# The second half of each low-part subtraction stays on the Pool engine up to the end of the cross attention

## The chip, the cores and the metric

One NeuronCore of a Trainium2 chip runs the whole program. The metric is the device time of one execution in microseconds (us); the number for a kernel is the median of its runs. Engine names are those of the profile: PE is the matrix engine (PEld its weight loads), DVE the vector engine, ACT the scalar engine, POOL the general-purpose engine, SP the engine that issues most of the transfers.

## What is computed

One layer of a transformer-like network on 256 tokens of 1024 channels, in float32:

```
x = layer_norm(ALPHA * x + token_mixer(x))        # three branches, gated and summed:
                                                  #   sparse attention, convolution, gated linear attention
x = layer_norm(ALPHA * x + cross_attention(x, mem))
x = layer_norm(ALPHA * x + moe_ffn(x))            # 32 experts, 4 for each token
```

The token mixer multiplies x by `w_in` (1024 x 6952), each branch's result by a 512 x 1024 matrix, and the gated sum by `w_out`; the cross attention has projections for queries, keys, values and its output. The experts hold 32 x 3 matrices' worth of 1024 x 1024 weights, 12 MB each expert.

## The kernel before

**Stages.** The program has a front, which is the token mixer and the cross attention, and then the experts. In the front every weight is used in blocks of 512 rows by 512 columns, 1 MB each, called slots here. A block comes by a transfer into one of six places of a ring (`fetch`, `R0 = 6`), is cut in two parts, and is multiplied by the activations, which are cut in two as well: three products stand for one float32 product (high times high, high times low, low times high).

**One slot** (`wslot`, line 121). The block `t` is [128, 4, 512]. It is handled in two halves, j = 0 (its first two chunks of 128 rows) and j = 2 (its last two). For each half ACT copies it to `wh` in a format of fewer bits, and then `t - wh` is written to `wl` by one subtraction of 128 x 1024 elements:

```
for j, eng in ((0, self.nc.vector), (2, self.nc.gpsimd if self.pooled else self.nc.vector)):
    js = slice(j, j + 2)
    self.copy(h[:, js, :n], t[:, js, :n])
    eng.tensor_tensor(out=l[:, js, :n], in0=t[:, js, :n], in1=h[:, js, :n].bitcast(F32), op=ALU.subtract)
```

The subtraction of the first half is always DVE's. That of the second half is POOL's where `self.pooled` is set, and DVE's elsewhere (line 142 in both cases). The first slot of the program (`quick`) and the two slots with `pair` don't take this path. `wh` and `wl` have two buffers each, so a slot's copies start when PE is done with the slot two before, and the slot before is multiplied meanwhile. The ring's place of `t` is free when the last of the four instructions has read it; SP then issues the next transfer into it.

**Where pooled is set.** It is 0 from the start, 1 for `nsa_in` (lines 1519 to 1521), whose four plain slots thus use POOL, and 0 again for all that follows: the three calls of `merge` (18 slots), `out_proj` with `w_out` (4), `keys`, `queries` and `values` (12), and `out_proj` with `xa_wo` (4, the last into the tiles `lasth`, `lastl`). That is 38 slots.

**Order.** The instructions of the front are put in an order for each engine by a planner that works through a modelled time: of what is ready on an engine, the one of the highest priority goes first, and program order gives the priority unless `high_priority` lifts it. The splitting of slots is lifted by 3000 places (`PRIO`), the softmaxes of the sparse attention by 6000. Each engine then works through its list strictly in order. From `route` on (line 853), after the slots of `xa_wo`, the order is that of the program.

**Beside the slots.** DVE does three quarters of the 31 taps of the convolution (line 320), with POOL the last quarter (lines 317 and 318), then the convolution's LayerNorm (PE lines 330, 337 and 342 with DVE lines 331, 343 and POOL's power on line 230), the sparse attention's softmaxes (lines 607 to 620), the merges (102, 689), and the LayerNorm after `w_out` (725, 237, 239, 229, POOL's power on 230, 243, 245). The transposes of that LayerNorm's rows on PE (line 91, `row`) lead to the queries. POOL also issues some transfers: the bias table `wide` (271), the LayerNorm's factors `gb` (207), the experts' biases `ye` (1036) and the router's weights `rw` (811). The experts' weights come by SP's queue on lines 1017 and 1024, the first of them while the front still runs, into places of the ring and into the front's memory as it becomes free.

Of the kernel before, what the change touches and what calls it, by code (L numbers as in the profile page):

```python
# [40 lines left out]
NEG = -1.0e30  # L41
# [5 lines left out]
# the first weights' column, in w_in  # L47
GATE0 = 1816
# the expert that comes first, and the place in the sequence of the last LayerNorm's preparation
FIRST = 16  # L50
MID = 20
# pieces of the last LayerNorm: (on DVE, tokens, columns), and of the output
# [4 lines left out]
class Rows:  # L57
    """[128 tokens, 2, 1024] in four tiles of 512 columns"""
# [12 lines left out]
class Front:  # L71
    """The two attention-like sublayers, up to the tokens that the experts see."""
# [23 lines left out]
    def gate(self, out, in_, scale=1.0):  # L96
        """out = 2 * sigmoid(scale * in_) - 1, from the table that has exp too"""
        return self.nc.scalar.activation(out, in_, AF.Tanh, scale=scale / 2)

    def gated(self, out, gate, in_):  # L100
        """out = 2 * sigmoid * in_"""
        self.nc.vector.scalar_tensor_tensor(out, gate, 1.0, in_, op0=ALU.add, op1=ALU.mult)

    def fetch(self, w, r0, c0, n, heads=False, parts=1):
        t = self.ring.tile([P, 4, 512], F32, name="w")
        at = 0
        for a, m in c0 if isinstance(c0, tuple) else ((c0, n),):
            if heads:
                # rows by (head of a group, group, channel)
# [11 lines left out]
    def wslot(self, w, r0, c0, n, pair=False, into=None, heads=False):  # L121
        """512 rows x n columns of a weight, as its 12-bit part and the rest."""
        t = self.ahead.pop() if self.ahead else self.fetch(w, r0, c0, n, heads)
        h, l = into or (self.wsp.tile([P, 4, 512], F32R, name=name) for name in ("wh", "wl"))
        if self.after:
            # the first weights are split after x
            self.copy(h[0:1, :, 0:1], self.after.pop().bitcast(F32))
        with self.tc.high_priority(offset=PRIO):
            if self.quick:
                # the first ones in parts, so that the products start early  # L130
# [14 lines left out]
    def project(self, w, c0, n, outs, x, nslots=2, pair=False, small=False, heads=False):  # L145
        """outs: (bank, offset, 'T', columns) gives [128 channels, 256 tokens];
        (bank, offset, 'N', columns, t) gives [128 tokens, channels]."""
# [3 lines left out]
        banks = []  # L151
# [28 lines left out]
    def projT(self, w, c0, x, nslots=2, pair=False, small=False, heads=False):  # L180
        """512 columns of x @ w, transposed: two banks of [128, 2, 256]."""
        return self.project(w, c0, 512, [(m // 2, (m % 2) * S, 'T', self.col(m * P)) for m in range(4)], x, nslots, pair, small, heads)
# [4 lines left out]
    def to_T(self, nat, nk, pool=None, name=None, into=None):  # L187
        """[128, 2, nk*128] tokens -> [128 channels, nk, 256] split in two."""
# [15 lines left out]
    def bcast_rows(self, dst, src):  # L204
        """every partition of dst gets the row src (n elements)"""
# [4 lines left out]
    def consts(self, cst, keep):  # L210
# [4 lines left out]
        # the PE's clock rises while x comes  # L215
# [10 lines left out]
    def rpow(self, pool, out, in_, eps, n):  # L226
        """out = (in_ + eps) ** -0.5 for [128, n]"""
# [4 lines left out]
    def norm(self, pool, r, out, gb):  # L232
        """LayerNorm of [128, 1024] rows"""
# [13 lines left out]
    def rel_table(self, pool):  # L247
        """skewed copies of the bias: wide[p, h, w] = bias of head h at distance 128 + p - w, NEG where negative"""
# [25 lines left out]
    def conv_cols(self, tmp, pool):  # L274
# [12 lines left out]
        # the taps meet twice the gated values  # L287
# [17 lines left out]
    def conv_out(self, pool):  # L305
        """the taps, a quarter of them on Pool, and the rest of the branch"""
# [73 lines left out]
    def misc_in(self, keep, pool):  # L380
        """the low-rank decay inputs (16) and the gates of the sparse attention (24)"""
# [44 lines left out]
    def gla(self, pool, opool):  # L426
# [5 lines left out]
        # the blocks of 64 on the diagonal  # L432
# [90 lines left out]
    def nsa_in(self, pool):  # L523
# [29 lines left out]
        # compressed keys and values  # L553
# [31 lines left out]
    def nsa(self, pool, opool, wide):  # L585
# [6 lines left out]
        def weights(t, br, g):  # L592
            """the softmax, times the gate"""
# [57 lines left out]
        # the softmax of a part runs before the one before it is turned  # L651
# [41 lines left out]
    def out_proj(self, w, o, enter=None, after={}, into=None):  # L693
        """o @ w, [128 tokens, 512] in bank t * 2 + c; the first tokens are ready before the others"""
# [27 lines left out]
    def residual(self, res, bank, t, c):  # L722
        """res = alpha * res + what the sublayer gave"""
# [9 lines left out]
    def four(self, out, banks, **kw):  # L733
        """two banks of a projection, channels first"""
# [15 lines left out]
    def weights(self, pool, q, kT, pr):  # L750
        """the softmax of the queries against the keys"""
# [38 lines left out]
    def mixed(self, xo, v, pt):  # L790
        """the values by those weights"""
# [11 lines left out]
class Moe:  # L803
# [3 lines left out]
    def prepare(self, cst, pool):  # L807
        """the router seen from rows r before their LayerNorm: logits = rs * (r @ gw - mean * sum(gw)) + (b @ rw + rb)"""
# [27 lines left out]
        # slots from 1 on  # L836
        self.io = cst.tile([P, P], F32, name="io")
        nc.gpsimd.iota(self.io[:], pattern=[[1, P]], base=1, channel_multiplier=0, allow_small_or_imprecise_dtypes=True)
        # rows of an expert, and of a half for each half of the columns
# [13 lines left out]
    def route(self, cst, wk, w, o, into, enter, r, x2h, row):  # L853
        """the last projection of the cross attention, LayerNorm of the rows r, which are in x1's place, but for the
        columns' factors and terms, and beside it what the router makes of them. Its result is in two parts; each tile
        of the second takes the place of the tile of r before it."""
# [32 lines left out]
        def scores(t):  # L889
            # in the PE's column groups, side by side  # L890
# [5 lines left out]
        def busy():  # L896
            """keeps the PE's clock up while it waits"""
# [15 lines left out]
        def largest(t):  # L913
            """the four largest of each token, equal ones by index"""
# [42 lines left out]
        # position of a token among its expert's, from 1; 0 for no token  # L957
# [23 lines left out]
    def residual(self, gb, x2):  # L981
        """the second LayerNorm's result again, for the sum; its factors and terms are brought from columns to rows"""
# [16 lines left out]
    def last_rows(self, gb, rows):  # L999
        """the last LayerNorm's factors and terms, for all partitions"""  # L1000
# [11 lines left out]
    def load(self, e, last=False):  # L1012
        """an expert's weights, in the order in which they are used: rows of w_gu by 128, then of w_down by 256"""
# [15 lines left out]
    def biases(self, pool):  # L1029
        """the experts' biases of g and u, for 128 rows = (half, part, expert)"""  # L1030
# [7 lines left out]
    def setup(self, cst):  # L1038
        """the biases of g and u in two exact parts"""
# [14 lines left out]
    # A block is a run of w slots (64 or 32) of one expert. The outputs' column chunks go to the PE's column groups.  # L1054
    # Slots 0..63 of two experts share the tiles of 128 rows: one gather and one sum for both.
# [7 lines left out]
    def onehot(self, pe, parts):  # L1063
        """slots' one-hot columns, [128 tokens, slots] twice; parts: (expert, first slot, count, column)"""
# [6 lines left out]
    def take(self, pe, xn, c):  # L1071
        """half of the channels of the slots' tokens"""
# [15 lines left out]
    def scaled(self, out, in_, d, on_dve):  # L1088
        """the LayerNorm's factors and terms, for the channels of a run of 128"""
# [6 lines left out]
    def gather_T(self, pe, xT, xT1, j):  # L1096
        """256 of the channels of the first four experts' slots, channels first"""
# [16 lines left out]
    def gates(self, pe, parts, tag="pg"):  # L1114
        """gated one-hot map of slots, in 128 columns; parts: (expert, first of pe's columns, column, count)"""
# [14 lines left out]
    def gates_of(self, e, pe, w):  # L1130
        """for a block that is summed alone: its rows are (column half, slot), with w = 32 all of it twice"""
# [8 lines left out]
    def up(self, e, W, blocks, gus, between=(), lag=0):  # L1140
        """blocks: (xT, w); w = 64: g and u in a bank each, [128 = (half, slot), 512]; w = 32: both in one,
        [128 = (g or u, half, slot), 512]; a second block may lag by some rows of 128"""
        nc = self.nc
        at = 4
# [3 lines left out]
        if blocks[-1][1] != CAP:  # L1148
            # the same for 64 rows, with 64 zeros on each side
# [32 lines left out]
    def act(self, gu, w, uc):  # L1182
        """(u + 1) * g * sigmoid(1.702 g), clamped, in two halves"""
# [41 lines left out]
    def down(self, W, blocks, between=()):  # L1225
        """blocks: (hT, w, bank); w = 64: [128 = (column half, slot), 512]; w = 32: (column half, part of the sum, slot)"""
# [12 lines left out]
    def combine(self, pgT, ye, alone=False, last=False):  # L1239
        """y += the slots' results, by gate; ye: rows are a pair's slots, or (column half, slot) of one block"""  # L1240
# [443 lines left out]
```

## Time and profile before

| what | value |
|---|---|
| median of 3 runs | 1567.79 us |
| the runs | 1559.61, 1567.79, 1568.36 us |
| the profiled execution: span from the first to the last instruction | 1554.9 us |
| span below the fastest run / below the median | 4.7 / 12.9 us |
| PE busy | 1371.5 us (88% of the span) |
| DVE busy | 547.6 us (35%) |
| ACT busy | 320.0 us (21%) |
| POOL busy | 136.6 us (9%) |
| subtractions on line 142 by DVE / by POOL | 98 / 4 |

The page gives the profiled execution by its span alone, so it is set against the runs by the difference in the table. Busy shares are means over stages of very different kinds; the rows below are therefore taken by stretches of the span. A matrix instruction's length in the rows is that from its start to its modelled end, and they overlap: the distance of their starts tells how fast PE goes.

### The profile page before, as it was taken

To read this page: it belongs to the slowest core of one execution; us is meant where nothing else is said; L and a number is where in the kernel's file an instruction comes from. 1 tells how busy PE (TensorE), PEld (TensorE's weight loads), DVE (VectorE), ACT (ScalarE), POOL (GpSimd) and SP (SyncE) were. 2 spreads that over 40 slices of the span, in tenths; PEclk is the share of its full clock that TensorE was granted. 3 is DMA by queue.
4 is the path that set the end of the run, shared out by engine and by line. 5 is a ranking of instruction groups with operands and counts; after the bars stand their busy time and mean duration, and the time that the engine had idled before them with its cause. 6 is when DMAs were issued, how large, how long until landed. Compare 5 with 4: busy or idle time off the path is not lost. (4 is left out here: it accounts for less than half of the span.)

```text
span 1554.9 us, 18456 instructions
## 1 busy us (share of the span) xinstructions
PE 1371.5 (88%) x7190; PEld 705.8 (45%) x7190; DVE 547.6 (35%) x1243; ACT 320.0 (21%) x638; POOL 136.6 (9%) x139
## 2 busy tenths in 40 slices
PE   8879999999999978887879788988888999988895
PEld 8768879998743323232322232223223332233332
DVE  5999785765431221111212121213122122112213
ACT  4424653445320111010101010101111011101100
POOL 3983000000110000000000000000030000000001
PEclk9989999999999998999999899999999999799998
DMA  9436536557789999989996789588889997699970
GB/s 308 138 94 152 188 82 215 205 186 273 273 310 404 414 416 402 405 346 374 365 391 240 297 361 409 220 341 348 355 324 388 417 409 323 252 360 396 384 295 29
DMA packets 110163, 469.93 MB, mean 302 GB/s; under 512 B 12081, under 2 KB 16276, under 8 KB 77244
## 3 DMA queue, kind: packets, MB, share of 16 engines
q1 hardware_dynamic: 108028, 462.53, 76.5%
q0 software_dynamic: 1712, 4.26, 1.3%
q8 instruction: 104, 1.70, 0.4%
q10 hardware_dynamic: 272, 1.05, 0.2%
q14 instruction: 47, 0.39, 0.1%
HBM read 466.49 MB, written 1.31 MB: 301 GB/s over the span
## 5 line engine op out<-in xcount | busy, mean ns | idle before, releaser
L1158 PE MATMUL g<-w,xT 128*64 128x512 f32 x1024 | 299.0, 638 | 52.2 <-issue 27.7
L1158 PE MATMUL u<-w,xT 128*64 128x512 f32 x1024 | 292.4, 619 | 11.4 <-issue 11.4
L1233 PE MATMUL m<-w,hT 128*64 128x512 f32 (+1 forms) x1120 | 253.0, 627 | 0.1
L1192 DVE TENSOR_SCALAR gc<-g 128x256 f32<-128x256 f32 x64 | 26.8, 419 | 520.3 <-PE g L1158 477.1
L1158 PEld LDWEIGHTS g<-w,xT 128*64 128x64 f32 x1024 | 77.7, 144 | 195.6 <-issue 188.2
L1158 PEld LDWEIGHTS u<-w,xT 128*64 128x64 f32 x1024 | 86.7, 144 | 165.6 <-issue 165.6
L1193 ACT ACTIVATE row<-gc 128x256 f32<-128x256 f32 (+1 forms) x70 | 29.1, 417 | 559.8 <-DVE gc L1192 559.8
L142 DVE TENSOR_TENSOR wl<-w,wh 128x1024 fp32r<-128x1024 f32 (+1 forms) x96 | 114.3, 1226 | 66.3 <-ACT wh L80 66.1
L1233 PEld LDWEIGHTS m<-w,hT 128*64 128x64 f32 (+1 forms) x1120 | 73.1, 139 | 134.7 <-issue 132.1
L80 ACT ACTIVATE wh<-w 128x1024 fp32r<-128x1024 f32 (+1 forms) x112 | 105.7, 990 | 101.3 <-PE big L172 65.5
L172 PE MATMUL big<-xh,wh 128*128 128x256 f32 x352 | 101.4, 288 | 0.0
L172 PE MATMUL big<-xl,wh 128*128 128x256 f32 x352 | 101.1, 287 | 0.0
L172 PE MATMUL big<-xh,wl 128*128 128x256 f32 x352 | 100.8, 288 | 0.0
L1401 DVE COPY ye<-m 64x512 f32<-64x512 f32 x32 | 22.2, 694 | 136.3 <-ACTq L1405 96.5
L172 PEld LDWEIGHTS big<-xl,wh 128*128 128x128 f32 x352 | 68.5, 195 | 1.1 <-issue 0.8
L172 PEld LDWEIGHTS big<-xh,wl 128*128 128x128 f32 x352 | 68.2, 194 | 1.2 <-issue 1.1
L172 PEld LDWEIGHTS big<-xh,wh 128*128 128x128 f32 x352 | 68.6, 195 | 0.2
L1244 PE MATMUL y<-ye,pgT 128*128 128x512 f32 x128 | 61.9, 628 | 4.0 <-ACTq L1410 4.0
L994 POOL TENSOR_TENSOR w<-w,row 128x512 f32<-128x512 f32 x4 | 5.2, 1316 | 641.6 <-PE u L1158 641.6
L1092 DVE TENSOR_SCALAR xT<-m,rowc 128x128 f32<-128x128 f32 x64 | 22.0, 403 | 107.3 <-PE m L91 98.9
L80 ACT ACTIVATE ye<-m 64x512 f32<-64x512 f32 x32 | 18.9, 590 | 167.8 <-PE m L1233 148.7
L91 PE MATMUL m<-ident,uc 128*128 128x128 f32 (+1 forms) x140 | 28.9, 289 | 23.9 <-ACT hT L80 20.2
(432 smaller groups left out, 1743.0 us busy)
## 6 DMA issues: line engine op xcount, KB each, us to landing
w<-in_expert_w_gu_dram SPq DMA_DIRECT2D x256, 1024.0 KB
w<-in_expert_w_down_dram SPq DMA_DIRECT2D x127, 1024.0 KB
w<-in_w_in_dram SPq DMA_DIRECT2D x23, 1024.0 KB
w<-in_xa_wkv_dram SPq DMA_DIRECT2D x8, 1024.0 KB
w<-in_w_branch_dram SPq DMA_DIRECT2D x4, 1024.0 KB
w<-in_w_out_dram SPq DMA_DIRECT2D x4, 1024.0 KB
w<-in_xa_wq_dram SPq DMA_DIRECT2D x4, 1024.0 KB
w<-in_xa_wo_dram SPq DMA_DIRECT2D x4, 1024.0 KB
```

The source lines that it names most:

```text
L80: self.nc.scalar.activation(out, in_, AF.Copy, scale=scale)
L91: self.nc.tensor.transpose(out, in_, self.ident[0:k, 0:k])
L142: eng.tensor_tensor(out=l[:, js, :n], in0=t[:, js, :n], in1=h[:, js, :n].bitcast(F32), op=ALU.subtract)
L172: self.last = nc.tensor.matmul(dst, l, r, start=(b not in seen), stop=(last and i == 2), skip_group_check=True)
L994: self.nc.gpsimd.tensor_tensor(out=x2[:, t, s], in0=self.x2h[:, t, s].bitcast(F32), in1=self.x2l[:, t, s].bitcast(F32), op=ALU.add)
L1092: self.nc.vector.tensor_scalar(out, in_, g, t, op0=ALU.mult, op1=ALU.add)
L1158: nc.tensor.matmul(dst, xT[:, k, :], W[k][:, c * 512:c * 512 + 512], start=(k == 0), stop=(k == 7 and at != 7), skip_group_check=True)
L1192: nc.vector.tensor_scalar_min(gc[0:n, s], g[:, s], 7.0)
L1193: nc.scalar.activation(sg[0:n, s], gc[0:n, s], AF.Sigmoid, scale=1.702)
L1233: self.nc.tensor.matmul(pd[p0:p0 + w, :], hT[:, j, h * w:h * w + w], W[8 + k][:, c * 512:c * 512 + 512], start=(i < P // (2 * w)), stop=(i ...
L1244: self.nc.tensor.matmul(self.y[t][c][:], pgT[rows, t, :], ye[rows, v, :], start=False, stop=last, skip_group_check=True)
L1401: nc.vector.tensor_copy(ye[c:c + CAP, 1, :], pd[CAP:P, :])
```

## The change

`f.pooled` is set before `nsa_in` as before and is no longer set back. From there to the end of the front every plain slot has the subtraction of its second half on POOL. The rest of the diff takes out comments and docstrings, so line numbers after 1521 fall by one.

```
         glas.close()
         f.pooled = 1
         f.nsa_in(nsa1)
-        f.pooled = 0
         ob = conv_end()
         nsap = ExitStack()
```

## Rows read from the trace of the kernel before

**Rows 1.** Busy time of each engine in stretches of the span (us from its start). The columns are: the stretch and its length; busy time of PE, PEld, DVE, ACT and POOL with their counts; the granted clock of PE as a share of full speed; the DMA share; GB/s. The stretches are the part before the first moved subtraction, the end of the convolution, the sparse attention, the merges and `w_out`, the first LayerNorm, the cross attention, the way to the experts, and the first experts.

```profile
50.00:141.00 91.00, 72.84 (x640) 64.44 (x639) 87.79 (x158) 33.57 (x62) 72.35 (x65) 0.92 0.37 101
141.00:172.00 31.00, 30.40 (x298) 29.57 (x296) 26.22 (x50) 11.55 (x15) 0.71 (x1) 1.00 0.95 265
172.00:233.00 61.00, 60.96 (x399) 46.90 (x398) 49.02 (x97) 39.45 (x126) 1.71 (x4) 1.00 0.30 87
233.00:308.00 75.00, 75.00 (x562) 71.93 (x560) 45.68 (x53) 31.50 (x38) 1.60 (x4) 1.00 0.65 211
308.00:330.00 22.00, 21.85 (x168) 20.74 (x167) 20.79 (x34) 11.45 (x16) 3.75 (x5) 1.00 0.58 192
330.00:398.00 68.00, 68.00 (x430) 61.76 (x430) 35.81 (x46) 34.00 (x53) 0.00 (x0) 1.00 0.66 241
398.00:436.00 38.00, 34.16 (x278) 26.97 (x278) 18.35 (x55) 11.73 (x19) 7.27 (x8) 0.96 0.72 281
480.00:560.00 80.00, 73.36 (x328) 26.94 (x324) 17.59 (x55) 8.69 (x20) 0.00 (x0) 1.00 1.02 416
```

**Rows 2.** Who waited for whom: PE's waits from 141 to 408 us, the only row there is (us in total, times, longest); then the longest of PE's waits from 560 to 900 us.

```profile
PE s L574 <- DVE cmy L102: 0.6, 1, 0.6
...
PE g L1158 <- DMA w<-in_expert_w_gu_dram: 21.9, 3, 7.6
```

**Rows 3.** Instructions grouped by line and shape, from 140 to 430 us on DVE: the subtractions of the slots after `nsa_in` (busy us, mean ns of one, idle time before them and who ended it).

```profile
L142 DVE TENSOR_TENSOR wl<-w,wh 128x1024 fp32r<-128x1024 f32 x74 | 87.5, 1220 | 57.9 <-ACT wh L80 57.7
...
L142 DVE TENSOR_TENSOR lastl<-w,lasth 128x1024 fp32r<-128x1024 f32 x2 | 2.4, 1222 | 1.6 <-ACT lasth L80 1.6
```

**Rows 4.** The instructions of POOL in order of time (start, length in us): its two subtractions of full size, in `nsa_in`.

```profile
108.49 2.52 POOL L142 TENSOR_TENSOR wl<-w,wh 128x1024 fp32r<-128x1024 f32 x1
...
121.19 3.24 POOL L142 TENSOR_TENSOR wl<-w,wh 128x1024 fp32r<-128x1024 f32 x1 [1.72 <-PE big L172]
```

**Rows 5.** The instructions of DVE in order of time, at those two places and just beside them.

```profile
108.73 2.56 DVE L466 TENSOR_TENSOR gx<-gq,gd 128x256 f32<-128x256 f32 x1
...
111.55 0.41 DVE L466 TENSOR_TENSOR gx<-gq,gd 128x256 f32<-128x256 f32 x1
...
122.18 2.94 DVE L320 SCALAR_TENSOR_TENSOR cy<-cu,cp,cy 128x256 f32<-128x256 f32 x2
...
125.11 0.47 DVE L320 SCALAR_TENSOR_TENSOR cy<-cu,cp,cy 128x256 f32<-128x256 f32 x1
```

**Rows 6.** A slot of the queries, in the calm part of the cross attention: ACT's two copies, DVE's two subtractions, and on PE the first product with that slot and the first with its second half.

```profile
342.81 2.01 ACT L80 ACTIVATE wh<-w 128x1024 fp32r<-128x1024 f32 x2 [3.25 <-PE big L172]
...
343.90 2.36 DVE L142 TENSOR_TENSOR wl<-w,wh 128x1024 fp32r<-128x1024 f32 x2 [3.38 <-ACT wh L80]
...
348.49 0.28 PE L172 MATMUL big<-xoh,wh 128*128 128x256 f32 x1
...
351.37 0.28 PE L172 MATMUL big<-xoh,wh 128*128 128x256 f32 x1
```

**Rows 7.** The end of the convolution: DVE's first and last subtractions there, its last taps, and what PE runs when the taps end (line 330 reads them).

```profile
141.14 2.35 DVE L142 TENSOR_TENSOR wl<-w,wh 128x1024 fp32r<-128x1024 f32 x2
...
159.79 2.85 DVE L320 SCALAR_TENSOR_TENSOR cy<-cu,cp,cy 128x256 f32<-128x256 f32 x7
...
163.16 2.35 DVE L142 TENSOR_TENSOR wl<-w,wh 128x1024 fp32r<-128x1024 f32 x2
...
161.90 1.99 PE L330 MATMUL s<-cy,omean 128*128 128x256 f32 x8
163.55 0.47 PE L172 MATMUL big<-xh,wh 128*128 128x256 f32 x1
```

**Rows 8.** The first LayerNorm: ACT's copies of the first keys' slot, DVE's subtractions and LayerNorm steps, PE's products with that slot's second half, and PE's first transposes of the LayerNorm's rows.

```profile
309.56 2.01 ACT L80 ACTIVATE wh<-w 128x1024 fp32r<-128x1024 f32 x2 [6.10 <-PE big L705]
...
311.25 4.62 DVE L142 TENSOR_TENSOR wl<-w,wh 128x1024 fp32r<-128x1024 f32 x4
...
319.28 2.35 DVE L142 TENSOR_TENSOR wl<-w,wh 128x1024 fp32r<-128x1024 f32 x2
321.55 0.74 DVE L243 SCALAR_TENSOR_TENSOR row<-res,mv,gb 128x512 f32<-128x512 f32 x1
322.21 1.41 DVE L245 SCALAR_TENSOR_TENSOR row<-row,rs,gb 128x512 f32<-128x512 f32 x2
...
315.09 0.28 PE L172 MATMUL s<-w,wl 128*128 128x256 f32 x1
...
323.66 1.47 PE L91 MATMUL s<-ident,row 128*128 128x128 f32 x12
```

**Rows 9.** The last slot of `xa_wo` before the order is the program's: ACT's copies, DVE's subtractions, SP's issue of the next experts' weights (start, us until the last of them is issued, count), and PE's first product that needs the slot's second half.

```profile
404.01 2.01 ACT L80 ACTIVATE wh<-w 128x1024 fp32r<-128x1024 f32 x2 [4.88 <-PE big L705]
...
405.10 2.36 DVE L142 TENSOR_TENSOR wl<-w,wh 128x1024 fp32r<-128x1024 f32 x2 [5.25 <-ACT wh L80]
...
407.49 15.78 SPq L1017 DMA_DIRECT2D w<-in_expert_w_gu_dram  x7
...
410.84 0.39 PE L705 MATMUL big<-wl,xoh 128*128 128x512 f32 x1
```

**Rows 10.** Two of POOL's instructions between the last slot of `nsa_in` and the router, in order of time, with the idle time before each and what ended it.

```profile
218.57 0.60 POOL L207 DMA_DIRECT2D gb<-in_norm_g_dram  x1 [47.82 <-DVE ns L607]
...
318.84 0.93 POOL L230 TENSOR_TENSOR rs<-rp,nhalf 128x1 f32<-128x1 f32 x1 [9.07 <-DVE rp L229]
```

More of the change, by code (lines that the diff above doesn't have):

```diff
@@ L1520, in hybrid_layer @@
         f.nsa_in(nsa1)
-        f.pooled = 0
         ob = conv_end()
```

## The prediction

> **What bounds the kernel now.** I read the busy time by stretches first, then PE's waits, then the instruction lists of DVE, ACT and POOL around the moved work. From 141 us on, where the first moved subtraction stands, to the end of the cross attention, PE is busy 30.40 of 31, 60.96 of 61, 75 of 75, 21.85 of 22 and 68 of 68 us, at full granted clock (1.00, 2.4 GHz) [rows 1]. That leaves 0.8 us of gaps in 257, and the only wait found there is 0.6 us [rows 2]. So this stretch is PE's; DVE, which gives work away, is busy 20.79 of 22 us at most. Whatever it gains is worth at most those 0.8 us to PE. Before 141 us PE does have gaps (72.84 of 91), with DVE at 87.79, but nothing in that part is moved. The question is then not what DVE saves, but whether the slower way through POOL makes PE wait where it never did.
>
> **What moves.** 38 subtractions: of DVE's 74 + 2 after `nsa_in` [rows 3] every second one. DVE loses 38 x 1.22 = 46 us of work. On POOL one such subtraction took 2.52 and 3.24 us [rows 4]; the longer one had DVE work beside it. I take 2.5 us, and 3.24 as the upper bound: 95 to 123 us of new work in about 266 us on an engine that is nearly idle there. Nothing is added in bytes, transfers or matrix work; SP's list of transfers stays, and nothing before 141 us is moved.
>
> **A slot in a calm place.** PE starts a slot at 348.49 and its second half at 351.37, so it needs 2.88 us for a half and 5.76 for a slot. ACT's two copies run from 342.81 to 344.82, DVE's first subtraction from 343.90 to 345.1, the second until 346.26 [rows 6]. With POOL the second half is ready at 345.1 + 2.5 = 347.6, with the upper bound at 348.3: 3.0 us or more before it is needed. 24 of the 38 slots stand in stretches like this (233 to 308, 330 to 398 us and the end). Cost 0; the cover is PE's own previous slot, and a POOL subtraction that comes over 3 us late uncovers it.
>
> **What DVE pays.** Here the rows speak against the change. While POOL did its 2.52 us from 108.49 on, a DVE instruction of 0.41 us with both operands in SBUF took 2.56; beside the 3.24 us from 121.19 on, two taps of 0.47 each took 2.94 together [rows 4, 5]. DVE thus stood still for 2.1 us each time, close to the whole of POOL's instruction. A moved subtraction gives DVE 1.22 us and takes up to 2.1: net 0.9 us lost where DVE has such an instruction next, 1.2 gained where it hasn't. In calm stretches DVE waits 3.4 us per slot [rows 6], and it doesn't matter. The Trainium skill, in "SBUF — State Buffer" (section "Who interferes with whom"), has it as a rule: a vector instruction with two SBUF inputs and a GpSimd instruction that reads SBUF exclude each other, and the second waits for the first to end. The trace agrees in both of these places. By that rule every subtraction moved into dense DVE work costs its full length; the time would then be the second rival's, 1589 to 1594 us, and not the 1574 of the sum below.
>
> **End of the convolution (141 to 172 us).** Here DVE is busy 26.22 of 31 us, with taps that all have two SBUF operands. Five slots start here, four before the taps end at 159.79 + 2.85 = 162.64 [rows 1, 7]. PE reaches the products that read the taps at 161.90 and goes on at 163.55 [rows 7]: just in time, with no slack. 4 x 0.9 = 3.5 us later taps are then 3.5 us of waiting. Ends: 0, if the planner puts those products behind further slots; 4 x 2.1 = 8.4 us, if the planner counts on a DVE that is freed and sets them earlier. I take +3.5, the difference of measured rows.
>
> **Sparse attention (172 to 233 us).** Five slots. DVE is busy 49.02 of 61 us [rows 1], so 12 us of idle time face 5 x 0.9 = 4.4 us, and many of its steps read PSUM for one operand. I take 0; ends 0 and 5 x 2.1 = 10.5 us. POOL's list has waits in it behind which moved work can now stand: the transfer of `gb` waits for the softmaxes until 218.57 [rows 10]. What it waits for is DVE, whose own first halves stand in the same order, so a subtraction behind it is seldom later than DVE's own half of that slot; I count nothing, and leave it to the upper end.
>
> **First LayerNorm (308 to 330 us).** The first slot of the keys is copied late (to 311.57), because `w_out` holds both buffers. DVE's first half ends at 312.4; POOL then needs until 314.9 to 315.6, and PE reaches that half at 315.09 [rows 8]: 0 to 0.5, I take 0.2. The second token half's LayerNorm ends at 323.6, and PE transposes its rows at 323.66, again with no slack. In that chain stand two subtractions at 319.28, one of which leaves (-1.2), while lines 243 and 245 have two SBUF operands and meet POOL's subtraction (+2.1); POOL's power at 318.84 may queue behind one (up to 2.5) [rows 8, 10]. Net +0.9, ends 0 and 3.4.
>
> **To the experts.** PE needs the last slot's second half at 410.84; DVE had it at 407.46, POOL has it at 406.1 + 2.5 to 3.2, at 409.3 at the latest: no wait. But the next experts' weights are issued at 407.49, right behind that subtraction [rows 9], and from 480 to 560 us the transfers fill the DMA engines (1.02 share, 416 GB/s) [rows 1]; PE later waits 21.9 us for weights [rows 2]. 1.2 us later start, +1.2; ends 0 and 1.8.
>
> **Sum.** 3.5 + 0 + 0.2 + 0.9 + 1.2 = +5.8 us. Against the profiled execution: 1554.9 + 5.8 = 1560.7 us of span. That span lies 12.9 us below the median of the runs shown, so the forecast for the median is 1567.8 + 5.8 = 1573.6, rounded to 1574 us. I call that no change to be told apart: a measurement of this kernel can tell about 1%, 15.7 us.
>
> **Rivals.** *All hidden* (chance 0.27): the calm slot holds everywhere, DVE makes up what it loses. For it: 12 idle us in the sparse attention, 3.4 per slot later. Against it: two places without slack. 1560 to 1568 us, by which of the runs before it resembles. *POOL holds DVE in the dense stretches* (0.19), slower: the ten slots between 141 and 233 us cost 2.1 us each, since PE's list is fixed for a DVE that is 1.2 us quicker per slot and PE waits in that order: 21 us, 1589. With the LayerNorm's 3.4 and the loads' 1.8 on top 1594; a lower granted clock after such pauses (0.92 in the stretch with 80% busy PE [rows 1]) could add a few us. It decides from 16 us, that is 7 or 8 slots fully uncovered. Against it: DVE's idle time in the second stretch. *DVE's relief counts* (0.05): softmaxes and taps end earlier, up to 46 us of DVE work gone. Against it: PE has 0.8 us of gaps to close; only a new order that also starts the experts' weights earlier could pass that. 1545 to 1557. *The change doesn't move the work* (0.02): against it, line 142 names the engine itself, and `nsa_in` shows POOL obeying. 1568.
>
> **Numbers.** The forecast of a few us has 0.47, from 1568 to 1583 us. The range reaches from the fastest run less the gaps and a little for the third rival (1557) to the second rival's upper sum (1594). Slower by over 1% (above 1583.5): the second rival 0.19 and a tail of the forecast 0.02, 0.21. Faster by over 1% (below 1552.1): half of the third rival and a little, 0.03. Within 1%: 0.76.
>
> **What would show it.** In the changed profile line 142 should show 42 POOL instructions of 2.5 to 3.3 us, and DVE's share of it 60. PE's waits from 141 to 330 us should show 3 to 6 us, named after DVE (lines 320, 331, 245), at the products on line 330 and at the transposes of `row`; PE waiting for POOL's `wl` should be below 1 us. The calm stretches should keep slots 5.76 us apart. I am wrong if PE waits for `wl` in the calm stretches (then POOL's list is blocked), if PE's waits from 141 to 233 us pass 15 us, or if the experts start earlier than before.

## The result, and the profile after

The changed kernel takes 1573.95 us (median of 12 runs, 1563.62 to 1581.84), the kernel before, run beside it, 1560.98 us (12 runs, 1553.93 to 1568.36). The ratio is 1.0075, with a 95% interval of [1.0047, 1.0102]: slower, by less than 1%. The forecast of 1574 us meets the number, but by two errors that cancel. The three runs on which it was based had a median of 1567.79, 6.8 us above what more runs give, and the sum of +5.8 us is half of the 11.7 us that the ratio stands for. The profiled executions are 17.4 us apart (1572.3 against 1554.9).

The windows of the stretches shown in [rows 1], of the changed kernel; the columns are those of [rows 1]. The last two lines cut the end of the convolution finer.

```profile
141.00:172.00 31.00, 24.82 (x227) 23.54 (x226) 25.06 (x43) 8.93 (x12) 13.12 (x8) 0.89 0.69 189
172.00:233.00 61.00, 59.27 (x390) 47.59 (x389) 41.56 (x82) 33.49 (x104) 13.44 (x8) 0.97 0.40 106
233.00:308.00 75.00, 74.99 (x580) 69.44 (x579) 42.71 (x42) 35.17 (x55) 31.35 (x17) 1.00 0.61 186
308.00:330.00 22.00, 21.54 (x106) 17.81 (x104) 16.16 (x23) 9.54 (x11) 10.23 (x6) 1.00 0.49 165
330.00:398.00 68.00, 67.05 (x483) 62.92 (x482) 31.02 (x47) 34.68 (x56) 33.05 (x16) 1.00 0.66 228
150.00:155.00 5.00, 3.08 (x18) 2.84 (x19) 4.89 (x17) 0.23 (x1) 0.00 (x0) 0.57 1.06 255
155.00:160.00 5.00, 5.00 (x35) 5.00 (x34) 2.95 (x6) 2.01 (x2) 0.56 (x1) 0.75 0.17 61
```

The stretches are cut by time, and the stages of the changed kernel stand up to 16 us later in them than in [rows 1]. At the end of the convolution PE was busy 30.40 of 31 us [rows 1] and is now busy 24.82, and the granted clock fell from 1.00 to 0.89. Right after a pause of PE (below) it is 0.57 and 0.75 in two stretches of 5 us, though PE works without a gap from 151.92 on: part of that work ran at 1.2 GHz instead of 2.4. The calm stretch from 233 to 308 us is as full as before.

PE's waits from 100 to 450 us of the changed kernel (us in total, times, longest), those of 141 us and later; [rows 2] showed a single one, 0.6 us at line 574. Waits of the router are left out, and of the 1.0 us for `wl` 0.2 lie before 141 us.

```profile
PE s L574 <- DVE cmy L102: 3.7, 1, 3.7
...
PE s L330 <- DVE cy L320: 1.6, 1, 1.6
...
PE s L91 <- DVE ns L620: 1.1, 1, 1.1
PE big L172 <- DVE wl L142: 1.0, 2, 0.8
PE s L91 <- ACT xkT L80: 0.9, 2, 0.7
...
PE s L645 <- ACT npt L80: 0.7, 1, 0.7
PE big L705 <- POOL wl L142: 0.4, 1, 0.4
```

PE hardly waits for POOL. It waits for DVE, or for ACT, while POOL is at work. The next three fences show why: DVE's list, POOL's list and PE's list of the changed kernel in order of time (start, length, count, and the idle time before with what ended it).

```profile
140.21 3.41 DVE L320 SCALAR_TENSOR_TENSOR cy<-cu,cp,cy 128x256 f32<-128x256 f32 x3
...
144.68 3.81 DVE L320 SCALAR_TENSOR_TENSOR cy<-cu,cp,cy 128x256 f32<-128x256 f32 x4
...
159.53 6.20 DVE L320 SCALAR_TENSOR_TENSOR cy<-cu,cp,cy 128x256 f32<-128x256 f32 x10
```

```profile
140.49 2.45 POOL L142 TENSOR_TENSOR wl<-w,wh 128x1024 fp32r<-128x1024 f32 x1 [2.09 <-ACT wh L80]
143.78 3.24 POOL L142 TENSOR_TENSOR wl<-w,wh 128x1024 fp32r<-128x1024 f32 x1 [0.83 <-ACT wh L80]
...
159.44 2.44 POOL L142 TENSOR_TENSOR wl<-w,wh 128x1024 fp32r<-128x1024 f32 x1 [11.94 <-ACT wh L80]
```

```profile
151.92 0.40 PE L574 MATMUL s<-cmy,cw 64*64 64x15 f32 x4 [3.75 <-DVE cmy L102]
...
164.99 1.99 PE L330 MATMUL s<-cy,omean 128*128 128x256 f32 x8 [1.59 <-DVE cy L320]
```

Seven taps in one go took 2.85 us in [rows 7], some 0.41 each. Beside POOL's subtraction three took 3.41 instead of 1.22, four 3.81 instead of 1.63, and ten 6.20 instead of 4.07: each time 2.1 to 2.2 us more. The last tap ends at 165.73, 3.1 us later than in [rows 7].

The same is seen behind the convolution, and not with taps alone. Beside POOL's subtractions line 85 took 2.69 us (1.22 in the kernel before). Lines 617 and 612, whose instructions have one tensor operand and not two, took 1.36 and 2.36 us instead of 0.16; the last is from `first_off` (below). In DVE's lists, first of the changed kernel, then of `first_off`:

```profile
185.78 2.69 DVE L85 SCALAR_TENSOR_TENSOR col<-cy,coh 128x1024 fp32r<-128x1024 f32 x1 [0.67 <-ACT coh L80]
...
225.98 1.36 DVE L617 TENSOR_SCALAR ncf<-ncf 128x4 f32<-128x4 f32 x1 [0.76 <-ACT nsc L615]
```

```profile
210.19 2.36 DVE L612 TENSOR_SCALAR nmx<-nmx 128x4 f32<-128x4 f32 x1
```

So two operands in SBUF are not the whole condition; no run here tests which single-operand instructions are held.

Subtractions on the whole page: as said ahead, about two in five are POOL's, at more than twice DVE's time.

```profile
L142 POOL TENSOR_TENSOR wl<-w,wh 128x1024 fp32r<-128x1024 f32 (+1 forms) x41 | 106.0, 2587 | 169.6 <-ACT wh L80 138.6
...
L142 DVE TENSOR_TENSOR wl<-w,wh 128x1024 fp32r<-128x1024 f32 (+1 forms) x59 | 72.9, 1248 | 70.6 <-ACT wh L80 70.5
```

**Milestones.** To place the loss I take the first product on three lines: 562 (it stands where the moved slots begin), 705 of `w_out`, and 763 (after the first LayerNorm and the queries). The view is that of one line's instructions: after the colon the shortest, median and longest in ns, then the first and the last start. First the kernel before, then the changed one.

```profile
L562 PE MATMUL s<-blk,w x64: 221/221/242, 141.2 to 143.0; 128*64 128x30 f32 x64
...
L705 PE MATMUL big<-wh,xh x32: 389/389/481, 290.2 to 311.4; 128*128 128x512 f32 x32
...
L763 PE MATMUL s<-xkT,xq x32: 377/379/483, 360.0 to 366.8; 128*128 128x256 f32 x32
```

```profile
L562 PE MATMUL s<-blk,w x64: 221/221/242, 141.5 to 143.3; 128*64 128x30 f32 x64
...
L705 PE MATMUL big<-wh,xh x32: 388/389/481, 304.4 to 326.3; 128*128 128x512 f32 x32
...
L763 PE MATMUL s<-xkT,xq x32: 377/379/483, 376.1 to 383.0; 128*128 128x256 f32 x32
```

From line 562 to `w_out`, which I call stretch A, 149.0 us became 162.9: +13.9. From `w_out` to line 763, stretch B, 69.8 became 71.7: +1.9. From there to the first expert product 75.2 became 74.2. So nearly all of the loss is in A. Its parts, from the fences above: waits at lines 574 and 330 (3.7 - 0.6 + 1.6 = 4.7 us), the other named waits in A (1.1 + 0.8 + 0.7 = 2.6), and the clock, (1 - 0.89) x 31 + (1 - 0.97) x 61 = 5.2 us at most, since PE stood still for a part of that time. That makes up to 12.5 of 13.9 us. The 0.8 is at 144 us, for a low part that DVE itself wrote late, behind the first taps that were held.

A and B come from one execution of each kernel. The start of A alone lies between 140.8 and 145.2 us in kernels that move nothing before it, and the clock falls in places where PE had waited for little or nothing: in `late_calm` and `none` (below) it is 0.97 and 0.93 in the sparse attention, with PE busy for 60.96 and 60.97 of 61 us (in `none` behind a wait of 0.5 us at 170 us). So the 0.89 goes with the pause of 3.75 us, while the 0.97 in the sparse attention, worth 1.8 us, is not shown to come from the change.

**A ruler finer than the median.** Runs of one kernel are spread by some 10 us either way. Each run has a granted clock beside its time, and within a kernel the two go together (correlation -0.89 to -0.98; 10 to 15 us for 0.01 of clock). A straight line through a kernel's runs, read at a clock of 0.950, leaves a scatter of 1 to 1.8 us. So read, the kernel before is at 1561.7 to 1561.9 us in three sets of 21 to 29 runs, the changed one at 1574.5: +12.7 us. This reading leaves out what a change does to the mean clock, so it is used beside the ratios and not in their place.

### The profile page after: what moved, and what is told of

It is laid out like the page before. It is cut to its first block, busy times and chain, and to the rows that moved or that the text cites. A ratio compares the mean times of both kernels' runs of the same rounds, so it can differ in the third digit from the quotient of the medians.

```text
span 1572.3 us, 18557 instructions
## 1 busy us (share of the span) xinstructions
PE 1376.9 (88%) x7190; PEld 708.1 (45%) x7190; DVE 530.1 (34%) x1205; ACT 320.4 (20%) x638; POOL 236.9 (15%) x177
## 5 line engine op out<-in xcount | busy, mean ns | idle before, releaser
L1158 PE MATMUL u<-w,xT 128*64 128x512 f32 x1024 | 294.2, 621 | 11.7 <-issue 11.7
L1233 PEld LDWEIGHTS m<-w,hT 128*64 128x64 f32 (+1 forms) x1120 | 72.8, 138 | 133.5 <-issue 130.5
L142 POOL TENSOR_TENSOR wl<-w,wh 128x1024 fp32r<-128x1024 f32 (+1 forms) x41 | 106.0, 2587 | 169.6 <-ACT wh L80 138.6
L142 DVE TENSOR_TENSOR wl<-w,wh 128x1024 fp32r<-128x1024 f32 (+1 forms) x59 | 72.9, 1248 | 70.6 <-ACT wh L80 70.5
```

Source lines behind the costliest of these rows:

```text
L1158: nc.tensor.matmul(dst, xT[:, k, :], W[k][:, c * 512:c * 512 + 512], start=(k == 0), stop=(k == 7 and at != 7), skip_group_check=True)
L1233: self.nc.tensor.matmul(pd[p0:p0 + w, :], hT[:, j, h * w:h * w + w], W[8 + k][:, c * 512:c * 512 + 512], start=(i < P // (2 * w)), stop=(i ...
```

## The experiments

Each edit is against the changed kernel. `f.pooled` decides, slot by slot as the program is laid out, who does the second subtraction. At the end a table has all results.

**Undo the first merge** (`first_off`): the six slots from the end of the convolution on go back to DVE, 32 stay with POOL.

```
         f.nsa_in(nsa1)
+        f.pooled = 0
         ob = conv_end()
...
+        f.pooled = 1
         f.merge(mgp, merged, 1, ob, False, False, None, None)
```

> POOL is left out of the six slots of the first merge (the stretch with the end of the convolution) and takes the second halves of the other 32 moved slots. Theory (POOL's subtraction holds DVE up in the stretch with the convolution's taps, PE then waits and loses its clock): PE's list up to the convolution's LayerNorm is that of before, the waits at lines 574 and 330 are 0.6 us and none again, the granted clock from 141 to 172 us is 1.00, and at most a third of the loss is left: 1.000 to 1.004 of the kernel before. Rival (the loss is spread over the later slots, the first LayerNorm and the later start of the experts' weights): 1.005 to 1.008.

**Only the first merge** (`first_only`): the six slots alone.

```
+        f.pooled = 0
         f.merge(mgp, merged, 1, ob, False, False, None, None)
```

> Only the six slots of the first merge have their second halves on POOL; the other 32 are DVE's again. Theory: nearly all of the loss is here, 1.005 to 1.008 of the kernel before, with PE's waits of 3 to 4 us at line 574 and 1 to 2 us at line 330 and a granted clock of about 0.9 from 141 to 172 us, as in the changed kernel. Rival (the loss is spread over the later slots): 1.000 to 1.003.

Measured: 1570.97 us, ratio 1.005 [1.0013, 1.0087], for `first_off`; 1568.12 us, 1.0044 [1.0013, 1.0074], for `first_only`. The windows at the end of the convolution and in the sparse attention, first of `first_off`, then of `first_only`:

```profile
141.00:172.00 31.00, 31.00 (x303) 30.22 (x302) 26.39 (x50) 11.71 (x16) 2.30 (x5) 1.00 0.99 274
172.00:233.00 61.00, 58.60 (x365) 44.29 (x365) 47.48 (x91) 35.69 (x120) 9.13 (x5) 0.97 0.17 55
```

```profile
141.00:172.00 31.00, 24.70 (x227) 23.42 (x226) 24.82 (x43) 8.93 (x12) 13.24 (x8) 0.89 0.68 193
172.00:233.00 61.00, 59.94 (x400) 48.95 (x399) 43.17 (x86) 33.70 (x104) 6.03 (x5) 0.97 0.40 105
```

PE's waits of `first_only`, for the same two lines as above:

```profile
PE s L574 <- DVE cmy L102: 3.7, 1, 3.7
...
PE s L330 <- DVE cy L320: 1.7, 1, 1.7
```

Without the six slots the end of the convolution is whole again; with them alone it shows the same loss as the changed kernel, with the same waits. PE's list is the same as in the changed kernel up to 220 us in `first_only`, and as in the kernel before up to 187 us in `first_off`. Stretch A is 153.7 us without the six and 160.9 with them alone, against 149.0 and 162.9: the six slots cost most, but the later slots, which I had put at nothing up to the LayerNorm, cost 2 to 5 us too (2 to 3 without the clock's share). Two of the six have their subtraction at 176 and 185 us, in the sparse attention; the wait of 1.1 us for `ns` and the clock of 0.97 there stand in `first_only` as well.

The whole times alone would not decide between the two expectations: 1.005 for `first_off` is the rival's figure and not the theory's 1.000 to 1.004, and 1.0044 for `first_only` lies between the theory's 1.005 and the rival's 1.003. Both are shifted by a pause in the experts, described below, that is long in `first_off` and short in `first_only`; this is why the split is read from A.

**Write, but don't read** (`write_only1` and `write_only`): the low parts of the second halves of the 38 slots are left out. POOL fills their place with zeros instead, once in the one and three times in the other, so that it takes 0.95 us, or about as long as the subtraction did.

```
-eng.tensor_tensor(out=l[:, js, :n], in0=t[:, js, :n], in1=h[:, js, :n].bitcast(F32), op=ALU.subtract)
+[eng.memset(l[:, js, :n].bitcast(F32), 0.0) for _ in range(3)] if j and self.pooled == 2 else eng.tensor_tensor(out=l[:, js, :n], in0=t[:, js, :n], in1=h[:, js, :n].bitcast(F32), op=ALU.subtract)
...
-        ob = conv_end()
+        f.pooled = 2; ob = conv_end()
```

(`range(1)` in `write_only1`.)

> As the changed kernel, but in the 38 moved slots POOL writes zeros into the second half instead of subtracting, so the low parts of those halves are left out and POOL reads nothing from SBUF. The lists of PE, DVE, ACT and SP are those of the changed kernel, instruction by instruction. Theory: DVE's taps take 0.47 us each beside POOL, PE's wait at line 574 is under 1.5 us, there is none at line 330, the clock from 141 to 172 us is 1.00, and the first product of the experts starts at 435 to 438 us (435.2 before, 450.3 in the changed kernel). Rival (the new order of PE's list itself costs the time): the waits stay at 3 us or more and the experts start at 446 us or later.

> As the run in which POOL writes zeros instead of subtracting, but it writes them three times, so that POOL is taken for 2.9 us per slot, somewhat longer than by the subtraction (2.4 to 2.8 us), and still reads nothing; the low parts of the second halves of the 38 slots are left out. Theory (the harm comes from POOL's reading while DVE reads two operands): DVE's taps beside POOL stay at 0.47 us, PE's wait at line 574 is under 1.5 us, and w_out's first product starts at 293 to 297 us (290.2 before, 304.4 in the changed kernel, 294.4 with one writing). Rival (the harm comes from the length of POOL's work, which makes the low parts late): PE waits for POOL's wl, 3 us or more in all, and w_out starts at 300 us or later.

The lists of DVE and of POOL of `write_only1` in order of time; its first line in each is a real subtraction in `nsa_in`, and what ran beside it:

```profile
108.93 2.56 DVE L466 TENSOR_TENSOR gx<-gq,gd 128x256 f32<-128x256 f32 x1
...
140.13 1.28 DVE L320 SCALAR_TENSOR_TENSOR cy<-cu,cp,cy 128x256 f32<-128x256 f32 x3
141.33 1.22 DVE L142 TENSOR_TENSOR wl<-w,wh 128x1024 fp32r<-128x1024 f32 x1
142.46 1.67 DVE L320 SCALAR_TENSOR_TENSOR cy<-cu,cp,cy 128x256 f32<-128x256 f32 x4
```

```profile
108.68 2.52 POOL L142 TENSOR_TENSOR wl<-w,wh 128x1024 fp32r<-128x1024 f32 x1
...
141.47 0.95 POOL L142 MEMSET wl<- 128x1024 f32 x1 [1.85 <-issue]
```

The granted clock is the last but two of the columns in the window of `write_only1` at the end of the convolution:

```profile
141.00:172.00 31.00, 30.39 (x288) 29.31 (x288) 22.32 (x47) 11.12 (x15) 6.94 (x10) 0.94 0.87 239
```

And of `write_only`, DVE's taps and the three fills on POOL beside them:

```profile
144.47 1.66 DVE L320 SCALAR_TENSOR_TENSOR cy<-cu,cp,cy 128x256 f32<-128x256 f32 x4
```

```profile
143.42 2.73 POOL L142 MEMSET wl<- 128x1024 f32 x3 [0.84 <-PE big L172]
```

Beside fills that last as long as a subtraction, four taps take 1.66 us and not 3.81, and PE's waits at lines 574 and 330 are back at 0.6 us and at most 0.7. Stretch A is 153.0 us with one fill and 151.7 with three. So it is not that POOL is busy for long, but that it reads from SBUF, which holds DVE. The lists of PE, DVE, ACT and SP are the same in `write_only1` as in the changed kernel, so no order is behind the difference of 162.9 - 153.0 = 9.9 of the 13.9 us, the larger part of the loss. In `write_only` the planner made another order (line 330 stands 14 places earlier on PE); it is the taps beside its fills that count, not its A. For the other 4.0 us of `write_only1` the new order of the lists is left, made for a DVE with less to do. That is by elimination, in one execution: up to 1.9 of them are clock (0.94), which fell though PE had waited for no more than 0.6 us. Two of my expectations for `write_only1` failed by this: a clock of 1.00, and a first expert product at 435 to 438 us, which came at 439.9. The Trainium skill, in "SBUF — State Buffer" (section "Who interferes with whom"), says that a vector instruction with two SBUF inputs contends with a GpSimd instruction that reads SBUF and not with one that only writes it. Both runs agree.

**No subtraction on POOL at all** (`none`, and again as `none_again`), and in addition all taps on DVE (`none_taps`):

```
-        f.pooled = 1
         f.nsa_in(nsa1)
```

```
-            eng = nc.gpsimd if m == 3 else nc.vector
+            eng = nc.vector
...
-            elif m == 3:
+            elif m > 3:
```

> POOL takes no subtraction at all, not even the four of the sparse attention's input. If POOL's subtraction holds DVE up wherever DVE is dense, the wait of 3.3 us of PE at line 477, which follows the first of them, goes to 1.3 us or less, and the kernel is 0.997 to 1.000 of before. Rival (there POOL's help was worth its price, since DVE is the slower engine up to 141 us): 1.002 to 1.006.

> POOL takes no subtraction of the front's weights, and DVE takes all taps of the convolution, POOL none. Theory: POOL's share of the taps (65 us of its time from 37 to 108 us) holds DVE's two-operand instructions up there as well; DVE's taps go from 0.67 to 0.41 us on the mean in that stretch, which gives back some 16 us against 12.7 us for the 31 taps that it takes over, so the kernel is 0.988 to 0.994 of before, at most 4 us better than without the taps' move. Rival (DVE is the bound of that stretch, and 12.7 us more work lengthens it): 0.997 to 1.004.

> The kernel without POOL's subtractions once more, beside the one that also moves the taps. Theory: 0.991 to 0.996 of before, as the first time. If the first result came from the chip it ran on, 0.997 to 1.002.

`none` takes 1551.76 us, ratio 0.9933 [0.9903, 0.9964], and 1553.01 us, 0.9956 [0.9934, 0.9979], when run again: faster than both kernels. But the reason is not the one I had in mind. Its front does lose the held instruction of [rows 5] (0.41 us again) and with it a part of PE's wait at line 477 (3.3 to 1.0 us), line 562 comes at 135.6 us instead of 141.2, and yet `w_out` starts at 289.4 instead of 290.2 and the first expert product at 433.5, and 434.7 when run again, against 435.2. Of the 5.6 us 4.8 are lost again before `w_out`, and hardly by waiting: the clock is 0.98 at the end of the convolution and 0.93 in the sparse attention, worth 0.6 + 4.3 = 4.9 us, with PE busy for 30.53 of 31 and 60.97 of 61 us (0.97 and 0.93 when run again). The first experts' results come at the same time to 0.6 us. The window of the sparse attention in `none`:

```profile
172.00:233.00 61.00, 60.97 (x366) 46.77 (x365) 46.13 (x94) 38.23 (x124) 1.14 (x2) 0.93 0.25 70
```

`none_taps` frees DVE still more early on (a tap takes 481 ns instead of 669), reaches line 562 at 120.0, and waits 7.0 us at line 330 for the taps that DVE now has to do: 1554.05 us, 0.9957 [0.9935, 0.9978], nothing beyond `none`. That is neither the theory's 0.988 to 0.994 nor the rival's 0.997 to 1.004; `none` itself came out faster than the 0.997 to 1.000 that I expected.

The gain of `none` is in the experts, in one place. PE's list in order of time there, first of the kernel before, then of the changed one, then of `none`:

```profile
585.12 1.98 PE L1158 MATMUL g<-w,xT 128*64 128x512 f32 x4 [7.17 <-issue]
```

```profile
598.92 1.98 PE L1158 MATMUL g<-w,xT 128*64 128x512 f32 x4 [7.39 <-issue]
```

```profile
579.68 1.08 PE L1158 MATMUL g<-w,xT 128*64 128x512 f32 x4 [1.88 <-issue]
```

A pause of 7.2 us, for which the profile names no cause, is 1.9 us in `none`, and the products after it run at once at their fast 1.08 us for four, not 1.98. The results of the experts before it are 0.2 us ahead of the kernel before, those of the next five after it 7.3 to 8.9 us. The same pause is long (7.1 to 7.4 us) in the profiles of the kernel before, the changed one, `first_off`, `write_only1` and `none_taps`, and short (1.8 to 2.0) in `first_only`, `write_only`, `none`, `none_again` and the two kernels below. It doesn't go with what is subtracted where. So it shifts whole times by some 8 us, and the cost of the moved slots has to be read from A and B.

**Late slots alone** (`late`, `late_calm`): POOL is used from the last merge on only, 26 slots; in `late_calm` without the four slots of the keys, 22. PE's list is that of the kernel before in both.

```
         f.nsa_in(nsa1)
+        f.pooled = 0
         ob = conv_end()
...
+        f.pooled = 1
         f.merge(mgp, merged, 0, oa, False, True, mh, ml)
```

```
+            f.pooled = 0
             k0 = f.keys(0, mem, small=True)
...
+        f.pooled = 1
         f.queries(xo, q)
```

> What it does: only the 26 slots from the last merge on (the sparse attention's own branch, w_out, keys, queries, values, xa_wo) have their second subtraction on POOL; the 12 slots before keep DVE. PE's list of instructions is the same as in the kernel before, so a difference of the front can't come from an order. Theory (POOL's reading holds DVE only where DVE's list is dense; the slots from the last merge on are covered by PE's own work, the first LayerNorm excepted): the first product of w_out within 1 us of the kernel before (290.2), the product that follows the first LayerNorm (line 763) 1 to 3 us later, because two LayerNorm steps and four key slots meet; at the same granted clock the time is 0 to 3 us above the kernel before. Rival (every moved slot costs, in proportion): 26/38 of the 12.8 us that the whole change cost at the same clock, +8 to +9 us, and w_out's first product 2 us or more later.

> What it does: as the run before, but the four slots of the keys, beside the first LayerNorm, keep DVE for both halves; 22 slots use POOL. PE's list is again that of the kernel before. Theory: no time at all, w_out's first product and line 763 within 0.5 us of the kernel before, and at the same granted clock -1 to +1.5 us. Rival (every moved slot costs): +7 us. A third possibility, that relief of DVE in calm stretches pays: line 763 earlier than before by over 0.5 us.

`late`: 1554.8 us, ratio 0.997 [0.9945, 0.9996]; A is 149.0 us, to the tenth that of the kernel before, B 72.8 (+3.0). `late_calm`: 1553.47 us, 0.9972 [0.9951, 0.9992]; A 150.5, B 70.8 (+1.0). Their times are below the kernel before, but both have the short pause. The slots from the last merge on thus cost A nothing; the +1.5 of `late_calm` comes with a clock of 0.97 in the sparse attention, where it moves nothing. In B the key slots cost 2.0 and the others 1.0, by one execution of each, more than the "no time at all" that I expected there. In `late` the first product of `w_out` comes at 294.2, outside the 1 us that I gave it, because A itself begins 4.0 us later in that execution (its clock from 100 to 141 us is 0.88, against 0.96 before). At equal clock the two are 1.2 and 3.5 us below the kernel before, where A, B and the pause together would make some 5 and 7; this rest is not accounted for. The rival, a price for each moved slot, would have shown +8 and +7 us.

How the keys cost it, in ACT's list of `late`, from the LayerNorm on:

```profile
329.44 0.31 ACT L80 ACTIVATE onesr<-ones 128x128 fp32r<-128x128 f32 x1 [4.56 <-DVE m L851]
329.96 0.31 ACT L80 ACTIVATE trir<-tri 128x128 fp32r<-128x128 f32 x1 [0.20 <-POOL tri L830]
330.17 0.58 ACT L80 ACTIVATE xkT<-s 128x512 f32<-128x512 f32 x1
```

PE's transposes of `row` then wait 1.3 and 0.65 us for ACT's copies of `xkT`. They don't wait for the LayerNorm, as I had it, but for copies that stand on ACT behind set-up work of the router, which now stands ahead of them and waits for POOL and DVE itself.

With the clock's share, (1 - clock) times the length of the two stretches from 141 to 233 us, taken out of A, the kernels that move nothing to POOL in A before the last merge stand together: 149.0 before and in `late`, 148.7 in `late_calm`, 148.9 in `none`. Then `write_only1` has 151.1, `first_off` 151.9, `first_only` 155.7 and the changed kernel 157.7.

The table of all kernels. "At 0.950" is the reading described above; A and B are in us; "562" is the start of A; "pause" is that at 578 us.

| kernel | moved slots | median us | at 0.950 | 562 | A | B | pause |
|---|---|---|---|---|---|---|---|
| before | 0 | 1560.98 | 1561.8 | 141.2 | 149.0 | 69.8 | 7.2 |
| changed | 38 | 1573.95 | 1574.5 | 141.5 | 162.9 | 71.7 | 7.4 |
| `first_off` | 32 | 1570.97 | 1567.7 | 142.2 | 153.7 | 71.8 | 7.1 |
| `first_only` | 6 | 1568.12 | 1566.6 | 141.2 | 160.9 | 69.8 | 1.8 |
| `late` | 26 | 1554.8 | 1560.6 | 145.2 | 149.0 | 72.8 | 1.9 |
| `late_calm` | 22 | 1553.47 | 1558.3 | 140.8 | 150.5 | 70.8 | 1.9 |
| `none` | 0 | 1551.76 | 1553.7 | 135.6 | 153.8 | 69.8 | 1.9 |
| `none_again` | 0 | 1553.01 | 1554.3 | 135.6 | 153.8 | 70.1 | 1.9 |
| `none_taps` | 0 | 1554.05 | 1554.6 | 120.0 | 164.5 | 70.0 | 7.3 |
| `write_only1` | (38, filled) | 1560.36, one run | | 141.4 | 153.0 | 70.0 | 7.3 |
| `write_only` | (38, filled) | 1561.86, one run | | 143.4 | 151.7 | 70.1 | 1.9 |

## Why the prediction was right or wrong

- **The bound.** Right. A PE with 0.8 us of gaps had nothing to gain from a freed DVE, and got nothing.
- **The move and its price on POOL.** Right: 41 subtractions on POOL of 2.59 us in the mean and 59 on DVE, where 42 and 60 were said (the trace has two fewer than the program); PE waits 0.4 us for POOL's `wl`.
- **The calm slot.** Right where it was said to hold, from 233 us on: PE is busy 74.99 of 75 us in the changed kernel, and `late` has A unchanged, though `late_calm` loses about 1 us in B.
- **What DVE pays.** Right in size. The 2.1 us of [rows 5] came back in three places at 2.1 to 2.2 us. That it is POOL's reading was shown by the runs that only write. The condition was too narrow: instructions with one tensor operand were held too, for 1.2 and 2.2 us.
- **End of the convolution, +3.5: the step that failed first.** The taps do end 3.1 us later, close to the 4 x 0.9 of the step. The step then took this for PE's loss, with the wait at line 330 alone. Two things came on top. The planner, which counts on a freed DVE, set the products of line 574 twelve places and those of line 330 forty-seven places earlier in PE's list; I had named that as what would lead to the upper end, and took the lower value all the same. The wait then fell mostly at line 574, which the step doesn't name, 3.1 us more than before, with 1.6 at line 330 and 0.8 for a low part that DVE wrote late: 5.5 us. And the pause of 3.75 us was followed by a lower clock, (1 - 0.89) x 31 = 3.4 us at most. In all 5.5 + 3.4 = 8.9 us, above the upper end of 8.4. Lost clock stood only in the second rival, as "a few us"; a term for it belonged in the sum. PE's waits from 141 to 330 us were to show 3 to 6 us and show 8.3.
- **Sparse attention, 0: the other step that failed.** The 12 idle us of DVE are an average over 61 us. In its dense places POOL held it (line 85: 2.69 us for 1.22), PE waited 1.1 us for `ns` and 0.7 for `npt`, and the clock was 0.97, 1.8 us. With A at +13.9 and 8.9 at the convolution's end, 5.0 us are left for this stretch. A part of them comes with the last two of the first merge's six slots, which stand here. `first_off`, which moves slots there and behind it but none at the convolution's end, lost 4.7 in A, 1.8 of it clock, and `late` shows that those behind the stretch cost A nothing. Without the clock, whose cause here is open, 2 to 3 us remain against the 0 of the step.
- **First LayerNorm, +1.1.** B grew by 1.9 us, within the ends. The way was another: ACT's `xkT` behind the router's set-up, not DVE's LayerNorm steps.
- **To the experts, +1.2.** Wrong: from line 763 to the first expert product it took 74.2 us after 75.2. The later issue of the weights doesn't show there, nor behind it: from the first expert's result to the fifth's it is 109.0 us in both.
- **The sum and the base.** Terms of about 9 + 5 + 2 - 1 = 15 stand against the 5.8 forecast. The front lost 15.1 us in the profiled executions (the first expert product at 450.3 after 435.2), the whole kernel 12.7 us at equal clock. The base was too high by 6.8 us, since three runs of a kernel whose runs spread over 15 us don't fix its median. That the time met the forecast was luck in this sense. Nor is it a change that can't be told apart, as the sum's last sentence has it: with 12 runs of each the interval is 0.3% to either side, and not 1%.
- **The rivals.** The mechanism was the one of the second rival, POOL holding DVE in the dense stretches with PE's list fixed for a freed DVE, at about 14 us in A where it said 21: the size lies between my sum and that rival's.

What stays open: what the pause at 578 us waits for, and which order in the sparse attention would lose nothing. No run here tried either.

## What to carry to other kernels

Before moving work from DVE to POOL, ask what DVE does beside it and not how idle it is on average: here POOL's subtraction, which reads SBUF, stopped a DVE instruction with two SBUF operands, and at times one with a single operand, for up to the 2 us that it lasts, so it is nearly free only where DVE's results aren't awaited (here 22 of 38 slots for about 1 us). The planner, which didn't know of this, put the consumers earlier as well, and a pause of 3.75 us on PE was followed by as much as 3.4 us of lost clock. And before a whole time is credited to an edit, look where along the program two traces part: here a step of some 8 us far behind the edit made a version look better than its front.

## What was not expected of the hardware

- POOL filling 128 x 1024 elements takes 0.95 us, against 2.5 us for the subtraction of the same size, and three fills in a row left DVE's taps at 1.66 us for four.
- One pause of 3.75 us on a PE that had been nearly full was followed by a granted clock of 0.57 and 0.75 in the two 5 us stretches from 150 to 160 us, in the second of which PE was busy for all 5 us. Work at 1.2 GHz shows in the row itself: four products of line 1158 take 1.98 us after the long pause and 1.08 us after the short one. A full PE doesn't keep the clock either: in `none` it is 0.93 over 61 us of which PE is busy for 60.97.
- The spread between runs of one and the same kernel goes nearly all with the granted clock: 10 to 15 us for 0.01 of it, with 1 to 1.8 us left over.
- DVE instructions of 128 x 4 elements with one tensor operand, 0.16 us elsewhere, took 1.36 and 2.36 us beside a POOL subtraction.
